# One hybrid decoder layer on one core: Strassen halves for the large input projections, token-row form everywhere

## The chip, the cores and the metric

The kernel runs on one core of one Trainium2 chip. The metric is the device time of one execution in microseconds, median over several executions of the same program. All inputs lie in the device's HBM, the weights (264 MB) among them, and stream through the core once.

## The reference, cut to what matters

One layer, 256 tokens, model width 2048, four branches of width 1024, everything in float32. `w_in` has 14 sections of 1024 columns, 324 columns of the indexer, and four gates of 2048 columns.

```python
xn = rms_norm(x, ln_g)
(a_q, a_k, a_v, a_g, c_b, c_c, c_h, c_g, s_q, s_k, s_v, s_g, m_q, m_g,
 i_q, i_k, i_w, r_a, r_c, r_s, r_m) = [xn @ w for w in cols]
y_a = moba_attention(a_q, a_k, a_v) * silu(a_g)              # causal, 8 heads of 128
y_c = c_b * short_conv(c_c * c_h, conv_w, conv_b) * silu(c_g)
y_s = dsa_attention(s_q, s_k, s_v, i_q, i_k, i_w) * silu(s_g)  # top 64 keys by the indexer
mk, mv = split(rms_norm(mem, mem_ln_g) @ w_mem_kv)
y_m = memory_attention(m_q, mk, mv) * silu(m_g)              # 4 heads of 256, 256 memory tokens
merged = (sigmoid(r_a) * (y_a @ w_branch[0]) + sigmoid(r_c) * (y_c @ w_branch[1])
          + sigmoid(r_s) * (y_s @ w_branch[2]) + sigmoid(r_m) * (y_m @ w_branch[3]))
out = rms_norm(x + merged @ w_out, final_g)
```

## The kernel before, in words

Each float32 product is made of three TensorE products of split numbers: a value is `hi` (its rounded part) plus `lo` (the rest), and hi·hi, hi·lo and lo·hi are accumulated in PSUM. The activations `x_hl` stay in SBUF in split form, the contraction (2048) on the partitions in 16 chunks `k` of 128. The weights come in tiles `raw` of 1 MB (128 partitions x 2048 numbers), each by one DMA of SP's queue (L115), into the pool `rawp` of 3 buffers. Each half of such a tile is cast by ACT to a `hi` (L99) and subtracted by DVE to a `lo` (L100); the pool `spl` holds four `hi` and four `lo` half tiles. TensorE (PE) follows.

There are two forms of a projection. In the transposed form (`project_t`, L132 and L133) the weights are the stationary operand and the tokens move: one matmul of 512 columns takes `hi` times both parts of the tokens, one of 256 columns takes `lo` times their hi; the two sums are added when they leave PSUM (`sum_t`, L149 and L150). It gives columns on the partitions, as the attention's q and k want them. In the token-row form (`project`, L156 to L158) the tokens are stationary and three matmuls of 512 weight columns move through; it gives tokens on the partitions. Before, `project_t` makes A_Q, A_K, A_G, C_B, C_C, C_H, C_G, S_Q, S_K, S_G, M_Q, M_G, the memory keys and the indexer; `project` makes the values (`to_values`), the gates of the branches ("r" in `merge_branch`), the branch outputs ("w") and the output projection ("o"). PSUM is divided into tags: `acc` 4 banks, `s` 2, `pp` and `yp` one each.

The program is written branch by branch: memory, S, A, C. A scheduler orders the instructions on each engine from there, so that a later projection's matmuls stand between those of an attention; semaphores keep data and buffers. The startup takes M_Q's first 512 columns while x arrives (`first_columns`), loads the memory (`load_mem`), squares x (`square_sums`, L180, with loads of its own through SP's queue), and then makes the memory keys (`to_heads("kt", w_mem_k, ...)`).

Of the kernel before, what the change touches and what calls it, by code (L numbers as in the profile page):

```python
# [12 lines left out]
ALU = mybir.AluOpType  # L13
# [32 lines left out]
def hybrid_kernel(ctx, tc, x, xT, mem, memT, ln_g, mem_ln_g, w_t, w_n, w_idx, conv_w, conv_b, w_mem_k, w_mem_v,  # L46
# [6 lines left out]
    rawp = ctx.enter_context(tc.tile_pool(name="rawp", bufs=3))  # L53
# [6 lines left out]
    def bank(name, tag="acc"):  # L60

        return banks.tile([P, NB], F32, name=name, tag=tag, bufs={"acc": 4, "s": 2}.get(tag, 1))
# [67 lines left out]
    def products_t(o, hi, lo, k, nk, act):  # L130

        nc.tensor.matmul(o, lhsT=hi, rhs=act(k), start=(k == 0), stop=False)  # L132
        nc.tensor.matmul(o[:, 1], lhsT=lo, rhs=act(k)[:, 0], start=False, stop=(k == nk - 1))  # L133

    def project_t(src, act):

        nk, c = src.shape[1:]
        acc = [halves(bank("acc")) for _ in range(0, c, P)]
# [6 lines left out]
    def sum_t(dst, acc, row=None, rows=P):  # L145

        for j, a in enumerate(acc):
            low = tmp.tile([P, T], F32, name="low")
            nc.scalar.copy(out=low[:rows], in_=a[:rows, 1])  # L149
            nc.vector.tensor_add(dst[:, j], a[:rows, 0], low[:rows])  # L150
            if row is not None:
                nc.vector.tensor_mul(dst[:, j], dst[:, j], row[:rows])
# [7 lines left out]
    def project(srcs, act, name, t_outer=False):  # L160

        nk = srcs[0].shape[1]
        acc = [[bank(name)[:, :src.shape[2]] for src in srcs] for t in range(2)]
        parts = [split_weights(src, src.shape[2]) for src in srcs]
        if t_outer:
            held = list(parts[0])
            steps = ((p, t, 0) for t in range(2) for p in held)
        else:
            steps = ((p, t, n) for k0 in range(0, nk, 4) for n in range(len(srcs))
                     for p in itertools.islice(parts[n], 4) for t in range(2))  # L170
        for (hi, lo, k), t, n in steps:
            a = act(k)[:, :, t * P:(t + 1) * P]
            products(acc[t][n], a[:, 0], a[:, 1], hi, lo, k == 0, k == nk - 1)
        return acc

# [37 lines left out]

    def to_gate(c0):
        dst = to_heads("gt", w_sec(c0), x_act)
        for b in range(2):
            s = dst[:, 4 * b:4 * b + 4]
            nc.scalar.activation(out=s, in_=s, func=AF.Silu)
        return dst

    def to_values(srcs, act, col=None):

        dst = big.tile([P, 2, W], F32, name="vv", tag="vv")
        for n in range(2):
            acc = project([srcs[n]], act, "v")
            for t in range(2):
                d = dst[:, t, n * NB:(n + 1) * NB]
                if col is None:
                    nc.scalar.copy(out=d, in_=acc[t][0])
                else:  # L230
                    nc.vector.tensor_scalar(d, acc[t][0], col[:, t:t + 1], None, op0=ALU.mult)
        return dst

    def gate_y(yp, gt, y, c):

        yt = tmp.tile([P, 2, T], F32, name="yt", tag="yt")
# [22 lines left out]
    def masked_attention(q, k, v, gt, mask):  # L259
        y = y_parts()  # L260
        scale = P ** -0.5
        yp = None
        for h in range(8):
# [27 lines left out]
            if h % 2 == 1:  # L291
                gate_y(yp, gt, y, h - 1)
        return y

    def memory_attention(q, k, v, gt):
        y = y_parts()
        scale = 256 ** -0.5
        for h in range(4):
# [26 lines left out]
            gate_y(yp, gt, y, 2 * h)  # L325
        return y


    def indexer_parts():
        acc = project_t(w_idx[:, :, 0:TB], x_act)  # L330
        iq = const.tile([P, 2, T], F32, name="iq")
        sum_t(iq, acc)
        acc = project_t(w_idx[:, :, TB:], x_act)
        ikw = const.tile([68, 1, T], F32, name="ikw")
        sum_t(ikw, acc, rows=68)
        ikw = ikw[:, 0]
        ikp = const.tile([P, 2, T], F32, name="ikp")
# [41 lines left out]
    def merge_branch(b, y, after=None):  # L379
# [5 lines left out]
        for j in range(2):  # L385
            sig = big.tile([P, 2, W], F32, name="sig", tag="m16b")
            for i in range(2):
                acc = project([w_n[GATES + 4 * b + 2 * j + i]], x_act, "r")
                for t in range(2):
                    nc.scalar.activation(out=sig[:, t, i * NB:(i + 1) * NB], in_=acc[t][0], func=AF.Sigmoid)  # L390
            for i in range(2):
                n = 2 * j + i
                acc = project([w_branch[b, n]], lambda k: y[:, k], "w")
                for t in range(2):
                    m = merged[:, t, n * NB:(n + 1) * NB]
                    g = sig[:, t, i * NB:(i + 1) * NB]
                    if first:
                        nc.vector.tensor_mul(m, acc[t][0], g)
                    else:
                        nc.vector.tensor_mul(g, acc[t][0], g)  # L400
                        nc.vector.tensor_add(m, m, g)
                if after is not None:
                    after(n, merged)


    def first_columns(c0, dst):

        src = w_t[FIRST[c0]:FIRST[c0] + 2].rearrange("b p k c -> p k b c")
        outs = [halves(bank("first", tag)) for tag in ("acc", "acc", "s", "s")]
        xraw = big.tile([P, KC, T], F32, name="xraw", tag="m16b")  # L410
        for k0 in range(0, KC, 4):
            raw = raw_tile(NB).rearrange("p k (b c) -> p k b c", b=2)
            n = 1 if k0 == 0 else 2
            for k in range(k0, k0 + 4, n):
# [3 lines left out]
                for i in range(n):  # L418
# [13 lines left out]
    first_columns(M_Q, q)  # L432
# [14 lines left out]
    for b in range(2, 4):  # L447
        acc = project_t(w_sec(M_Q)[b], x_act)
        load_mem(b - 2)
        sum_t(q[:, 2 * b:2 * b + 2], acc)  # L450
    for t in range(2):
        square_sums(x, t, x_ss)
    x_col, x_row = inv_rms(x_ss, "x")
    nc.vector.tensor_mul(q, q, rows(x_row, 8))
    for b in (2, 3):
        load_mem(b)
    def normalize(b):
# [4 lines left out]
        nc.vector.tensor_mul(xn, xn, rows(x_row, 4))  # L462
        split(x_hl[:, ks, 0], x_hl[:, ks, 1], xn)

    k = to_heads("kt", w_mem_k, m_act, normalize)
    m_col, m_row = inv_rms(m_ss, "m")
    nc.vector.tensor_mul(k, k, rows(m_row, 8))
    v = to_values([w_mem_v[0], w_mem_v[1]], m_act, m_col)
    gt = to_gate(M_G)
    y = memory_attention(q, k, v, gt)  # L470
    idx = indexer_parts()
    merge_branch(BR_M, y)


    mask_s = indexer(*idx)
    q = to_heads("qt", w_sec(S_Q), x_act)
    k = to_heads("kt", w_sec(S_K), x_act)
    v = to_values([w_n[V_S], w_n[V_S + 1]], x_act)
    gt = to_gate(S_G)
    y = masked_attention(q, k, v, gt, mask_s)  # L480
    merge_branch(BR_S, y)


    q = to_heads("qt", w_sec(A_Q), x_act)
    k = to_heads("kt", w_sec(A_K), x_act)
    v = to_values([w_n[V_A], w_n[V_A + 1]], x_act)
    gt = to_gate(A_G)
    y = masked_attention(q, k, v, gt, mask_a)
    merge_branch(BR_A, y)


    cc = to_heads("qt", w_sec(C_C), x_act)
    u = big.tile([P, 8, T + 2], F32, name="u", tag="kt")
    nc.gpsimd.memset(u[:, :, 0:2], 0.0)
    for b in range(4):
        acc = project_t(w_sec(C_H)[b], x_act)
        us, cs = u[:, 2 * b:2 * b + 2, 2:], cc[:, 2 * b:2 * b + 2]
        sum_t(us, acc)
        nc.vector.tensor_mul(us, us, cs)
# [6 lines left out]
    bt = to_heads("vv", w_sec(C_B), x_act)  # L506
    for b in range(2):
        s = slice(4 * b, 4 * b + 4)
# [97 lines left out]
```

## Time and profile before

| | us |
|---|---|
| median of 3 runs | 1422.03 (1420.96 to 1423.45) |
| the profiled execution | 1421.22 |
| its span, first to last instruction | 1419.4 |
| PE busy, of the span | 1402.2 (99%) |
| DVE busy | 829.2 (58%) |
| ACT busy | 698.6 (49%) |
| mean granted TensorE clock | 0.995 |

The profile lists one execution. "Busy" of PE is modelled from pipelined matmuls: a single one is listed with 0.39 us though the next begins 0.23 us later, so the pitch from start to start is the cost. The chain of waits is the path followed back from the last instruction. A window gives the busy time of each engine in a stretch.

### The profile page before, as it was taken

The numbers are of one execution on the slowest core, as the hardware profiler recorded it, in microseconds if no ns is written. First come the engines' busy times: TensorE is split into PE (matmuls) and PEld (weight loads), VectorE is DVE, ScalarE is ACT, GpSimd is POOL, SyncE is SP. The second block draws the span as 40 slices with busy tenths as digits, with TensorE's granted clock in tenths as the row PEclk, the third lists the DMA queues.
The fourth block names the chain that finished last, engine by engine and source line by source line (L and its number), as shares of the span: only waits on it lengthen the run. The fifth ranks groups of instructions, "written<-read, shape, count | busy, mean of one in ns | idle before, by whom it ended". The sixth has DMA issues, their size and how long they took to land.

```text
span 1419.4 us, 18005 instructions
## 1 busy us (share of the span) xinstructions
PE 1402.2 (99%) x7168; PEld 1189.8 (84%) x7168; DVE 829.2 (58%) x1080; ACT 698.6 (49%) x960; POOL 10.8 (1%) x25
## 2 busy tenths in 40 slices
PE   9799999999999999999999999999999999999997
PEld 8688888888888888888888888888888888888887
DVE  7775546685554446764555446764557655455654
ACT  7644356644444447734444456844444445434443
POOL 1000000000000000000000000000000000000000
PEclk9899999999999999999999999999999999999999
DMA  9765544555555555455555554455555666555553
GB/s 316 277 214 201 180 138 178 178 178 183 198 183 181 202 181 172 154 178 196 189 181 193 189 181 175 152 183 199 182 193 189 207 217 224 184 191 193 178 188 109
DMA packets 49956, 269.27 MB, mean 190 GB/s; under 512 B 6656, under 2 KB 17456, under 8 KB 19024
## 3 DMA queue, kind: packets, MB, share of 16 engines
q1 hardware_dynamic: 48960, 264.03, 54.9%
q0 software_dynamic: 624, 3.31, 0.6%
q8 instruction: 56, 0.92, 0.3%
q10 hardware_dynamic: 288, 0.79, 0.1%
q14 instruction: 28, 0.23, 0.0%
HBM read 265.88 MB, written 2.10 MB: 189 GB/s over the span
## 4 chain that ended last, share of the span: by engine, by line
PE 97%; DMA 1%; issue 0%; ACT 0%; DVE 0%; POOLq 0%; POOL 0%; DVEq 0%; SPq 0%; ACTq 0%
PE acc L132 27%; PE acc L133 14%; PE r L157 8%; PE r L156 8%; PE r L158 8%; PE w L157 4%; PE w L158 4%; PE w L156 4%; PE v L158 3%; PE v L157 3%; PE v L156 3%; PE o L158 2%; PE o L157 2%; PE o L156 2%; PE first L132 1%; DMA raw<-in_w_mem_k 1%
## 5 line engine op out<-in xcount | busy, mean ns | idle before, releaser
L100 DVE TENSOR_TENSOR lo<-raw,hi 128x1024 fp32r<-128x1024 f32 (+1 forms) x496 | 594.6, 1201 | 505.9 <-ACT hi L99 504.4
L99 ACT CAST hi<-raw 128x1024 fp32r<-128x1024 f32 (+1 forms) x496 | 510.4, 1032 | 585.1 <-PE acc L132 212.9
L132 PE MATMUL acc<-x_hl,hi 128*128 128x512 f32 x1520 | 537.2, 398 | 0.0
L133 PE MATMUL acc<-x_hl,lo 128*128 128x256 f32 x1520 | 427.5, 282 | 0.0
L132 PEld LDWEIGHTS acc<-x_hl,hi 128*128 128x128 f32 x1520 | 285.4, 188 | 70.5
L133 PEld LDWEIGHTS acc<-x_hl,lo 128*128 128x128 f32 x1520 | 284.8, 187 | 0.6
L157 PE MATMUL r<-lo,x_hl 128*128 128x512 f32 x512 | 201.8, 394 | 0.0
L156 PE MATMUL r<-hi,x_hl 128*128 128x512 f32 x512 | 201.2, 394 | 0.0
L158 PE MATMUL r<-hi,x_hl 128*128 128x512 f32 x512 | 201.1, 393 | 0.0
L156 PEld LDWEIGHTS r<-hi,x_hl 128*128 128x128 f32 x512 | 96.3, 188 | 19.9
L158 PEld LDWEIGHTS r<-hi,x_hl 128*128 128x128 f32 x512 | 96.3, 188 | 19.6
L157 PEld LDWEIGHTS r<-lo,x_hl 128*128 128x128 f32 x512 | 96.4, 188 | 19.1
L157 PE MATMUL w<-lo,y 128*128 128x512 f32 x256 | 100.0, 392 | 0.0
L158 PE MATMUL w<-hi,y 128*128 128x512 f32 x256 | 98.8, 392 | 0.0
L156 PE MATMUL w<-hi,y 128*128 128x512 f32 x256 | 98.4, 391 | 0.0
L149 ACT COPY low<-acc 128x256 f32<-128x256 f32 (+1 forms) x103 | 38.4, 374 | 76.7 <-PE acc L133 76.7
L157 PEld LDWEIGHTS w<-lo,y 128*128 128x128 f32 x256 | 48.1, 188 | 9.7
L158 PEld LDWEIGHTS w<-hi,y 128*128 128x128 f32 x256 | 48.1, 188 | 9.7
L156 PEld LDWEIGHTS w<-hi,y 128*128 128x128 f32 x256 | 48.0, 188 | 9.5
L158 PE MATMUL o<-hi,mt 128*128 128x512 f32 (+1 forms) x160 | 55.4, 347 | 0.0
L157 PE MATMUL o<-lo,mt 128*128 128x512 f32 (+1 forms) x160 | 55.2, 346 | 0.0
L156 PE MATMUL o<-hi,mt 128*128 128x512 f32 (+1 forms) x160 | 55.0, 344 | 0.0
(186 smaller groups left out, 1226.4 us busy)
## 6 DMA issues: line engine op xcount, KB each, us to landing
raw<-in_w_t SPq DMA_DIRECT2D x92, 1024.0 KB, 5.2
raw<-in_w_n SPq DMA_DIRECT2D x80, 1024.0 KB, 4.9
raw<-in_w_branch SPq DMA_DIRECT2D x32, 1024.0 KB, 5.1
raw<-in_w_out SPq DMA_DIRECT2D x16, 1024.0 KB, 4.9
raw<-in_w_mem_k SPq DMA_DIRECT2D x8, 1024.0 KB, 7.1
raw<-in_w_mem_v SPq DMA_DIRECT2D x8, 1024.0 KB, 4.8
raw<-in_w_t SPq DMA_DIRECT2D x16, 256.0 KB, 5.7
raw<-in_memT SPq DMA_DIRECT2D x2, 1024.0 KB, 6.2
```

The source lines that it names most:

```text
L99: nc.scalar.copy(out=hi, in_=src)
L100: nc.vector.tensor_sub(out=lo, in0=src, in1=hi.bitcast(F32))
L132: nc.tensor.matmul(o, lhsT=hi, rhs=act(k), start=(k == 0), stop=False)
L133: nc.tensor.matmul(o[:, 1], lhsT=lo, rhs=act(k)[:, 0], start=False, stop=(k == nk - 1))
L149: nc.scalar.copy(out=low[:rows], in_=a[:rows, 1])
L156: nc.tensor.matmul(o, lhsT=ah, rhs=hi, start=start, stop=False)
L157: nc.tensor.matmul(o, lhsT=ah, rhs=lo, start=False, stop=False)
L158: nc.tensor.matmul(o, lhsT=al, rhs=hi, start=False, stop=stop)
```

## The change

The contraction of 18 column blocks of 1024 is cut (S_Q, S_K, S_V, A_Q, A_K, A_V, C_C, C_H, C_G, C_B, and two blocks of each of the four branch gates). Chunks 0 to 7 are taken as a 2 x 2 by 2 x 2 product of blocks (two token halves, two contraction quarters, two column halves) by seven products of 12 matmuls (m1, m5, m6, m7, z, x, y) where eight stood; chunks 8 to 15 stay plain. The sums of activations are made once (`sums_of`, into `x_sums`). The sums of weights are made for each block: `bs` = b11 + b12' is a load of SP (L177) onto which a DMA of POOL's queue accumulates a second quarter (L183); DVE adds b22 onto it (L243) and later b21 (L258). `b12` is made by a load and a second accumulating DMA. Seven results pass through adds of DVE (L246, L250 to L252, L264, L270) and one copy of ACT (L239). Such a block is called a unit below.

All blocks but M_Q, the memory keys and the indexer now have the token-row form. Those that feed heads are transposed afterwards by PE (`transposed`, L334, 16 transposes of 128 x 128 for a section), and the output gates are applied after the attention (`gated`). The transposed form that is left takes three matmuls of 256 columns (L133 to L135). `rawp` has 4 buffers, PSUM's tags are `a` and `b` with 2 banks each in the place of `acc`. At the startup the squares of x, its normalization and half the memory's loads are written beside the memory keys.

```diff
-    rawp = ctx.enter_context(tc.tile_pool(name="rawp", bufs=3))
+    rawp = ctx.enter_context(tc.tile_pool(name="rawp", bufs=4))
...
     def products_t(o, hi, lo, k, nk, act):
-        nc.tensor.matmul(o, lhsT=hi, rhs=act(k), start=(k == 0), stop=False)
-        nc.tensor.matmul(o[:, 1], lhsT=lo, rhs=act(k)[:, 0], start=False, stop=(k == nk - 1))
+        a = act(k)
+        nc.tensor.matmul(o, lhsT=hi, rhs=a[:, 0], start=(k == 0), stop=False)
+        nc.tensor.matmul(o, lhsT=hi, rhs=a[:, 1], start=False, stop=False)
+        nc.tensor.matmul(o, lhsT=lo, rhs=a[:, 0], start=False, stop=(k == nk - 1))
...
+    def quarter_sum(src1, src2, k0, k1):
+        raw = quarter(src1, k0)
+        nc.gpsimd.dma_start(out=raw, in_=src2[:, k1:k1 + 4], accum_op=ALU.add)
+        return raw
...
+    def by_halves(srcs, act, sums, nat, done):
...
+        b11 = quarter(srcs[0], 0)
+        m1 = bank("m1", tag)
+        product(m1, a(0, 0), b11, True, True)
+        bs = quarter_sum(srcs[0], srcs[1], 0, 0)
+        nc.scalar.copy(out=n00, in_=m1)
+        m5 = bank("m5", tag)
+        product(m5, s(0), bs, True, True)
+        b22 = quarter(srcs[1], 4)
+        nc.vector.tensor_add(bs, bs, b22)
+        m6 = bank("m6", other)
+        product(m6, s(1), bs, True, True)
+        nc.vector.tensor_add(n01, m6, n00)
+        b12 = quarter_sum(srcs[1], srcs[1], 0, 4)
+        m7 = bank("m7", tag)
+        product(m7, s(2), b12, True, True)
+        nc.vector.tensor_add(n10, m7, n01)
+        nc.vector.tensor_add(n01, m5, n01)
+        nc.vector.tensor_add(n11, m5, n10)
+        z = bank("z", other)
+        product(z, s(3), b22, True, False)
+        r = bank("r", other)
+        plain((z, r), act, srcs[1], 8, (False, True), False)
+        b21 = quarter(srcs[0], 4)
+        nc.vector.tensor_add(bs, bs, b21)
+        y = bank("y", tag)
+        x = bank("x", tag)
+        product(x, a(1, 1), bs, True, False)
+        plain((z, r), act, srcs[1], 12, (False, False), True)
+        for t, (o, i) in enumerate(((n01, z), (n11, r))):
+            nc.vector.tensor_sub(out=o, in0=i, in1=o)
+            done(t, 1, o, False)
+        product(y, a(1, 0), b21, True, False)
+        for k0 in (8, 12):
+            plain((y, x), act, srcs[0], k0, (False, False), k0 == 12)
+        for t, (o, i) in enumerate(((n00, y), (n10, x))):
+            nc.vector.tensor_add(o, i, o)
+            done(t, 0, o, False)
...
+    def columns(c0, nat, done, halved, srcs=None):
...
+        if halved:
+            return by_halves(srcs, x_act, x_sums, nat, done)
...
-    for t in range(2):
-        square_sums(x, t, x_ss)
...
+    beside = {0: [lambda: square_sums(x, 0, x_ss)], 1: [lambda: square_sums(x, 1, x_ss), x_norm],
+              2: [lambda: normalize(0), lambda: load_mem(2)], 3: [lambda: normalize(1), lambda: load_mem(3)]}
...
+    q = to_heads("qt", S_Q, True)
+    k = to_heads("kt", S_K, True)
+    v = to_values(S_V, True)
+    masked_attention(q, k, v, mask_s)
+    finish(BR_S, S_G, q, True)
```

Where the orders stand against each other, three places matter. The first is DVE in the middle of the C branch, before, where C_H follows C_C (`lo` is half a weight tile, `qt` and `u` the two sections' sums):

```order
L100 TENSOR_TENSOR lo_8571<-raw_8548,hi_8570 128x1024 [waits PE_49,Activation_49]
L150 TENSOR_TENSOR qt_8133<-acc_8411,low_8499 128x256 [waits Activation_49]
L100 TENSOR_TENSOR lo_8602<-raw_8599,hi_8601 128x1024 [waits DMAHW2_49,PE_49,Activation_49]
L100 TENSOR_TENSOR lo_8622<-raw_8599,hi_8621 128x1024 [waits PE_49,Activation_49]
L100 TENSOR_TENSOR lo_8644<-raw_8641,hi_8643 128x1024 [waits DMAHW3_49,PE_49,Activation_49]
L150 TENSOR_TENSOR u_8502<-acc_8504,low_8590 128x256 [waits Activation_49]
```

The same engine at the same place after the change, from the last quarter of C_C's unit into C_H's (`raw_8644` is C_H's `bs`, `raw_8669` its b22, `raw_8694` its b12, `uu` C_C's result, `ch` C_H's):

```order
L100 TENSOR_TENSOR lo_8650<-raw_8644,hi_8649 128x1024 [waits DMASW0_49,Activation_49]
L270 TENSOR_TENSOR uu_8312<-y_8472,uu_8312 128x512 [waits PE_49]
L270 TENSOR_TENSOR uu_8312<-x_8473,uu_8312 128x512 [waits PE_49]
L100 TENSOR_TENSOR lo_8660<-raw_8644,hi_8659 128x1024 [waits Activation_49]
L243 TENSOR_TENSOR raw_8644<-raw_8644,raw_8669 128x2048 [waits DMAHW7_49,DVE_49]
L100 TENSOR_TENSOR lo_8674<-raw_8644,hi_8673 128x1024 [waits PE_49,Activation_49]
L100 TENSOR_TENSOR lo_8684<-raw_8644,hi_8683 128x1024 [waits PE_49,Activation_49]
L100 TENSOR_TENSOR lo_8699<-raw_8694,hi_8698 128x1024 [waits DMASW1_49,Activation_49]
L100 TENSOR_TENSOR lo_8709<-raw_8694,hi_8708 128x1024 [waits Activation_49]
L100 TENSOR_TENSOR lo_8723<-raw_8669,hi_8722 128x1024 [waits Activation_49]
L246 TENSOR_TENSOR ch_8620<-m6_8672,ch_8620 128x512 [waits PE_49]
```

Between the subtractions there now stand adds that wait for PE's end of the last unit (L270) and an add of a whole tile (L243), and two of the subtractions wait for an accumulating DMA (DMASW0, DMASW1). PE after the change, where m6 and m7 of C_H's unit meet:

```order
L154 MATMUL m6_8672<-hi_8673,x_sums_1518 128x512 [waits Activation_49]
L155 MATMUL m6_8672<-lo_8674,x_sums_1518 128x512 [waits DVE_49]
L156 MATMUL m6_8672<-hi_8673,x_sums_1518 128x512
L154 MATMUL m6_8672<-hi_8673,x_sums_1518 128x512
L155 MATMUL m6_8672<-lo_8674,x_sums_1518 128x512
L156 MATMUL m6_8672<-hi_8673,x_sums_1518 128x512
L154 MATMUL m6_8672<-hi_8683,x_sums_1518 128x512 [waits Activation_49]
L154 MATMUL m7_8697<-hi_8698,x_sums_1518 128x512 [waits Activation_49]
L155 MATMUL m6_8672<-lo_8684,x_sums_1518 128x512 [waits DVE_49]
```

The first matmul of m7, on the cast of the accumulated b12, has come to stand ahead of m6's last five. SP's loads for the same unit, with the buffers' releases they wait for:

```order
L177 DMA raw_8621<-in_w_n 128x2048 [waits DMAHW5_49,DMAHW2_49,DVE_49]
L177 DMA raw_8644<-in_w_n 128x2048 [waits DMAHW1_49,DVE_49]
L177 DMA raw_8669<-in_w_n 128x2048 [waits DMAHW7_49,DMAHW3_49,DVE_49]
L177 DMA raw_8694<-in_w_n 128x2048 [waits DMAHW4_49,DVE_49]
L177 DMA raw_8743<-in_w_n 128x2048 [waits DMAHW5_49,DVE_49]
L177 DMA raw_8777<-in_w_n 128x2048 [waits DMASW1_49,DVE_49]
```

Before, each load stood alone for its tile; now the loads of `raw_8644` and `raw_8694` are followed by an accumulation on POOL's queue, and the load of b21 (`raw_8777`) waits for the second of these.

## Rows read from the trace of the kernel before

**Rows 1.** Page, parts 1 and 4: busy time of each engine; the chain by engine.

```profile
PE 1402.2 (99%) x7168; PEld 1189.8 (84%) x7168; DVE 829.2 (58%) x1080; ACT 698.6 (49%) x960; POOL 10.8 (1%) x25
PE 97%; DMA 1%; issue 0%; ACT 0%; DVE 0%; POOLq 0%; POOL 0%; DVEq 0%; SPq 0%; ACTq 0%
```

**Rows 2.** Windows: us, busy time and instructions of PE, PEld, DVE, ACT, POOL; PEclk, DMA share, GB/s.

```profile
40.00:80.00 40.00, 31.75 (x169) 27.09 (x168) 29.24 (x38) 25.52 (x36) 1.46 (x2) 0.87 0.74 265
560.00:600.00 40.00, 40.00 (x208) 33.94 (x207) 30.69 (x69) 31.03 (x68) 0.00 (x0) 1.00 0.46 152
1200.00:1240.00 40.00, 40.00 (x177) 32.90 (x176) 17.55 (x15) 19.13 (x20) 0.00 (x0) 1.00 0.63 221
```

**Rows 3.** Timeline of PE at 985 us, row form: start, us, engine, line, operation.

```profile
985.34 0.39 PE L158 MATMUL r<-hi,x_hl 128*128 128x512 f32 x1
...
988.07 0.39 PE L158 MATMUL w<-hi,y 128*128 128x512 f32 x1
```

**Rows 4.** Timeline of PE at 43 us, transposed form.

```profile
43.51 0.40 PE L132 MATMUL acc<-x_hl,hi 128*128 128x512 f32 x1
43.74 0.28 PE L133 MATMUL acc<-x_hl,lo 128*128 128x256 f32 x1
...
49.16 0.40 PE L132 MATMUL acc<-x_hl,hi 128*128 128x512 f32 x1
```

**Rows 5.** Timeline of PE at 561 us, 256-column matmuls inside a row-form projection.

```profile
561.38 0.28 PE L252 MATMUL s<-part 128*128 128x256 f32 x1
561.50 0.28 PE L253 MATMUL s<-part 128*128 128x256 f32 x1
561.62 0.39 PE L157 MATMUL r<-lo,x_hl 128*128 128x512 f32 x1
```

**Rows 6.** Chain of waits at 207 us: start, us, what (transposes of the memory attention).

```profile
207.23 0.44 PE pp L317 x4
```

**Rows 7.** Chain of waits, startup.

```profile
42.44 6.88 DMA raw<-in_x
49.40 2.01 ACT raw L180 x2
51.43 7.57 DMA raw<-in_w_mem_k
```

**Rows 8.** Windows of the startup; columns as in rows 2.

```profile
52.00:60.00 8.00, 0.43 (x2) 0.19 (x2) 6.15 (x8) 5.82 (x9) 1.14 (x2) 0.66 0.90 320
60.00:70.00 10.00, 9.88 (x45) 8.52 (x46) 9.84 (x10) 6.29 (x8) 0.00 (x0) 0.76 0.58 204
```

**Rows 9.** Timelines at 59 and 997 us: operations in pairs, and a wait of PE.

```profile
59.02 2.00 ACT L99 CAST hi<-raw 128x1024 fp32r<-128x1024 f32 x2 [1.31 <-DMA raw<-in_w_mem_k]
60.10 2.36 DVE L100 TENSOR_TENSOR lo<-raw,hi 128x1024 fp32r<-128x1024 f32 x2
60.12 1.22 PE L132 MATMUL acc<-m16a,hi 128*128 128x512 f32 x2 [7.22 <-ACT hi L99]
...
996.85 1.28 DVE L400 TENSOR_TENSOR sig<-w,sig 128x512 f32<-128x512 f32 x2
```

**Rows 10.** Groups of DVE by form: xcount | busy, mean ns | idle before.

```profile
L100 DVE TENSOR_TENSOR lo<-raw,hi 128x1024 fp32r<-128x1024 f32 x476 | 582.0, 1225 | 498.6 <-ACT hi L99 497.3
L400 DVE TENSOR_TENSOR sig<-w,sig 128x512 f32<-128x512 f32 x24 | 15.7, 684 | 1.2 <-PE w L158 1.2
L504 DVE SCALAR_TENSOR_TENSOR qt<-u,cw,qt 128x256 f32<-128x256 f32 x16 | 6.7, 479 | 0.0
L502 DVE TENSOR_SCALAR qt<-u,cw,cb 128x256 f32<-128x256 f32 x8 | 3.0, 410 | 0.1
L454 DVE TENSOR_TENSOR qt<-qt,x_row 128x2048 f32<-128x2048 f32 x1 | 2.3, 2292 | 0.0
```

**Rows 11.** Waits: engine and tile, released by: us in total, times, longest.

```profile
DVE lo L100 <- ACT hi L99: 504.4, 402, 4.1
ACT hi L99 <- PE acc L132: 212.9, 131, 2.6
```

**Rows 12.** A queue (packets, MB, share of 16 engines); DMA issues (x, KB, us to landing).

```profile
q1 hardware_dynamic: 48960, 264.03, 54.9%
raw<-in_w_n SPq DMA_DIRECT2D x80, 1024.0 KB, 4.9
xr<-in_x POOLq DMA_DIRECT2D x2, 1024.0 KB, 6.5
```

**Rows 13.** Window in which the loads run closest; columns as in rows 2.

```profile
20.00:26.00 6.00, 6.00 (x38) 5.31 (x37) 3.29 (x6) 2.63 (x6) 0.00 (x0) 1.00 1.05 414
```

More of the change, by code (lines that the diff above doesn't have):

```diff
@@ L143, in project_t, with copy_t @@
         return acc
-    def sum_t(dst, acc, row=None, rows=P):
+    def copy_t(dst, acc, rows=P):
         for j, a in enumerate(acc):
[L148 to L152, printed above, removed]
+            nc.scalar.copy(out=dst[:, j], in_=a[:rows])
     def products(o, ah, al, hi, lo, start, stop):
@@ L158, in products, with project @@
         nc.tensor.matmul(o, lhsT=al, rhs=hi, start=False, stop=stop)
[L160 to L164, printed above, removed]
+    def project(src, act, name, t_outer=False):
+        nk, c = src.shape[1:]
+        tag = next(turn)
+        acc = [bank(name, tag)[:, :c] for t in range(2)]
+        parts = split_weights(src, c)
@@ new lines, in kept, with done, through, times @@
+    def kept(nat):
+        def done(t, n, src, psum):
+            if psum:
+                nc.scalar.copy(out=part(nat, t, n), in_=src)
+        return done
+    def through(nat, func):
+        def done(t, n, src, psum):
+            nc.scalar.activation(out=part(nat, t, n), in_=src, func=func)
+        return done
+    def times(nat, dst):
+        def done(t, n, src, psum):
+            nc.vector.tensor_mul(part(dst, t, n), src, part(dst, t, n))
+        return done
+    def transposed(nat, done):
+        for c in range(0, 8, 2):
+            pp = halves(bank("tp", "s"))
+            for i in range(2):
+                for t in range(2):
+                    nc.tensor.transpose(pp[:, i, t * P:(t + 1) * P], nat[:, t, (c + i) * P:(c + i + 1) * P], ident)
+            done(c, pp)
@@ L377, in hybrid_kernel, with gate_columns, merge @@
     state = {"merged": None}
[L379 removed]
+    def gate_columns(b, j, halved):
+        sig = nat_tile("sig")
+        columns(None, sig, through(sig, AF.Sigmoid), halved, [w_n[FIRST[R_0] + 4 * b + 2 * j + n] for n in range(2)])
+        return sig
+    def merge(b, j, sig, y, after=None):
         first = state["merged"] is None
@@ L466, in hybrid_kernel @@
+    k = big.tile([P, 8, T], F32, name="kt", tag="kt")
+    for b in range(4):
+        acc = project_t(w_mem_k[b], m_act)
+        for step in beside[b]:
+            step()
+        copy_t(k[:, 2 * b:2 * b + 2], acc)
     m_col, m_row = inv_rms(m_ss, "m")
     nc.vector.tensor_mul(k, k, rows(m_row, 8))
[L468 to L475, printed above, removed]
@@ new lines, in hybrid_kernel, with finish @@
+    for n in range(2):
+        acc = project(w_mem_v[n], m_act, "v")
+        normalize(2 + n)
+        for t in range(2):
+            nc.vector.tensor_scalar(part(v, t, n), acc[t], m_col[:, t:t + 1], None, op0=ALU.mult)
+    x_sums = big.tile([P, 4, 4, 2, P], F32R, name="x_sums", tag="m16b")
+    sums_of(lambda k0, n: x_hl[:, k0:k0 + n], x_sums)
+    memory_attention(q, k, v)
+    def finish(b, gate, val, halved, after=None):
+        y = to_gate(gate, val, False) if gate is not None else val
+        for j in range(2):
+            merge(b, j, gate_columns(b, j, halved), y, after)
@@ L493, in hybrid_kernel @@
+    columns(C_H, nat, times(nat, uu), True)
     u = big.tile([P, 8, T + 2], F32, name="u", tag="kt")
     nc.gpsimd.memset(u[:, :, 0:2], 0.0)
[L495 to L499, printed above, removed]
+    transposed(uu, lambda c, pp: nc.scalar.copy(out=u[:, c:c + 2, 2:], in_=pp))
+    cc = big.tile([P, 8, T], F32, name="cc", tag="qt")
     for c in range(8):
```

264 lines of the change are left out of this document (141 added, 123 removed).

## The prediction, made before the changed kernel ran

> **What bounds the kernel now.** I read the page first: PE is busy 99% of the span, and 97% of the chain that ended last is PE [rows 1]. Windows say where it is not: in 40 to 80 us PE is busy 31.75 of 40 us, elsewhere 40.00 of 40, with DVE at 30.69 in an attention stretch and 17.55 in a quiet one [rows 2]. So outside the startup a matmul taken away is time taken away, as long as the two engines that prepare weights keep ahead. The waits show that they do: DVE's subtraction waits 504.4 us for ACT's cast, which in turn waits 212.9 us for PE to give its buffer back [rows 11]. DVE and ACT idle because PE is slow, and the question is whether they still do after the change.
>
> **PE's work.** Prices are pitches, start to start. Row form: 12 matmuls between 985.34 and 988.07 us, 2.73 us, so 0.2275 each [rows 3]. Transposed form: 16 pairs in 43.51 to 49.16 us, 5.65 us, 0.353 a pair [rows 4]. A 256-column matmul takes 0.12 [rows 5], a transpose 0.44 / 4 = 0.11 [rows 6].
> - 18 units lose 12 of 192 matmuls: 18 x 12 x 0.2275 = -49.1 us.
> - 11 column blocks go from 128 pairs (45.2 us) to 192 row-form matmuls (43.7 us): -1.5 x 11 = -16.5 us.
> - 9 sections get 16 transposes: 144 x 0.11 = +15.8 us.
> - 304 pairs that stay transposed (M_Q 128, memory keys 128, indexer 48) become three matmuls of 0.12: 304 x 0.007 = +2.1 us.
>
> PE's work: -47.7 us, 3.4%.
>
> **Startup.** Before, SP issues the x loads and the memory loads ahead of the memory keys: the chain goes through x (6.88 us), its squares on ACT (2.01) and then the first key weights (7.57) [rows 7], and PE is busy 0.43 us in 52 to 60 us. In the 10 us after it, its granted clock is 0.76 [rows 8], a mean between its two levels, 1.2 and 2.4 GHz. The change moves the squares with their two loads, the normalization and two memory loads beside the key projections; the key weights go out behind the first half of the memory. Idle 7.6 us and 10 x (1 - 0.76) = 2.4 us at a low clock: -10 us. The moved steps are not free: each load is one more place in SP's queue (1 MB in 2.53 us at 414 GB/s [rows 13]), and DVE and ACT do the same work later, beside 180 us of matmuls that leave DVE idle. Next late would be the key weights themselves; ends 0 and -10, I take -10, since the chain names just the loads that go. `sums_of` adds two tile-half adds, four smaller ones and four splits, some 7 us of DVE once, beside the memory attention: nothing.
>
> **DVE in a unit.** Two casts in a row take 2.00, one 1.05, so a step of 0.95; two subtractions take 2.36 [rows 9], a lone one 1.225 [rows 10], so a step of 1.14. A 128x512 operation takes 0.684 alone [rows 10] and two take 1.28, so a step of 0.60 [rows 9]; a 128x2048 operation 2.29 [rows 10], less the same 0.08 in a row, 2.21. Per block before: 16 x 1.14 = 18.2 of 43.7 us. Per unit now: 22 x 1.14 + 2 x 2.21 + 8 x 0.60 = 34.3 of 180 x 0.2275 = 41.0 us. It still fits, by 6.7 us. But it is not even. The order excerpt of DVE shows what stands between the end of one unit and m6 of the next: two adds that wait for PE's last matmul (1.2), the second half of m5 (1.14), the add of b22 (2.21), then ACT's cast (1.05) and the subtraction (1.23): 6.8 us. PE has m1 and m5 in that time and the first matmul of m6, 25 x 0.2275 = 5.69. Stall per unit: 1.1 us, with semaphores (0.06 between cast and subtraction's start [rows 9]) 1.3. Everything queued behind the add of b22 on DVE (both halves of m6, then of m7) shifts with it; who waits is PE.
>
> Ten units are quiet. Eight have other DVE work in them: the first units of S and A (indexer, transposes' copies), the gates beside the attentions, and C_G with the convolution, 16 x 0.479 + 8 x 0.410 = 10.9 us [rows 10], 4.2 more than the spare. I take 4 us for each of the eight, with ends of 1.3 (it hides) and 8 (it comes in a lump in front of m6): 10 x 1.3 + 8 x 4 = **+45 us**, ends 23 and 77.
>
> ACT per unit: 22 x 0.95 and some 1 us of copies, 22 of 41 us: nothing, its cover is PE's 41.
>
> **The DMA chain.** Before, loads take 54.9% of 16 engines [rows 12]. A unit brings 9 loads and 2 accumulations, 11 MB in 41 us, 27.8 us at the closest pace of 2.53: no bandwidth problem. It's the latency: in SP's order b12's load goes into a buffer that comes free about 8.6 us before the unit's m1 (counted along the order with the pitches above); it lands 4.9 us or more after its issue [rows 12], about 1.2 us before m1, as it shares the engines with its neighbours; only then does POOL's accumulation go out. PE needs m7's cast, by the order excerpt in the middle of m6, 31 matmuls and the stall after m1's start: 7.05 + 1.2 - 1.05 for the cast = 7.2 us. No accumulating DMA exists before. The nearest row is POOL's plain load of 1 MB, 6.5 us [rows 12]: it would land about 4.9 us after m1 (4.7 to 5.3, as the load lands), 2.3 us to spare. That's one end. The other: an accumulation moves twice the data (old and added operand both read), 6.5 + 2.5 = 9.0 us; and because `bs`'s accumulation stands before it on POOL's queue, and its buffer delays the load behind it, b12 is late by twice 2.5 = 5.0, which is 2.7 us beyond the spare. The 10 units that stand back to back pay it: **+27 us**; the eight gate units follow 96 to 192 plain matmuls and don't. A price below that of the plain load has nothing for it: it also writes 1 MB. I take 9.0, since an add must read what it adds to.
>
> The Trainium skill has a rule that speaks here ("Collectives: The Full Stack", section "The bandwidth ceiling: the fold count and why AG ≠ RS ≠ AR"): a reducing transfer needs two source reads on one ring, and was measured 62.28 / 32.35 = 1.93 times slower than a copy. No run of before shows it; it is a rule on rings between cores. By it alone an accumulation would be an estimated 1.93 x 2.53 = 4.9 us of engine time, which gives the second end again.
>
> Also on POOL's in-order queue: 36 accumulations, each of which waits for its load; the indexer's two 64 KB copies and the x loads for the end stand behind them, both with 40 us or more before they're needed: nothing. The output's gate now comes after the attention and the transposes stand before "w"; a gate unit stands between, so nothing.
>
> **Sum.** Against the profiled execution, 1421.2 us (0.8 under the median): 1421.2 - 47.7 - 10 + 45 + 27 = 1435.5; **1436 us** against the median, 1% slower. About 0.2% is what a measurement of this kernel can tell from no change.
>
> **Rivals.**
> - A, *accumulation at the plain price*: b12 lands 2.3 us ahead of need, the +27 goes; 1421.2 - 47.7 - 10 + 45 = 1409 us, faster. With all of DVE's extra work hidden (23): 1387. It decides at an accumulation of about 7.7 us, (2 x (7.7 - 6.5) = the spare of 2.3). For it: the DMA engines are half idle [rows 12], and a second read can run beside the write. Against: the load behind which it queues already takes 4.9 us where 2.53 is the pace.
> - B, *the DMA queues become the bound*: 264.03 MB are 252 loads of 1.049 MB; 54.9% of 1419.4 us [rows 12] over 252 is 3.09 us of engine time each, 0.56 more than the 2.53 of the closest window. With 13 passes for a unit (9 loads, 2 accumulations of two) that is 40.2 of 41 us: no lost microsecond is caught up. b12 comes behind five passes of its unit and its own load, 6 x 0.56 = 3.4 us later, in all 18 units: 1435.5 + 60 = 1495 us. Against: in the startup 414 GB/s were reached [rows 13].
> - C, *the startup doesn't shrink*: the key weights were late because the memory itself was; +10 on any of the above. It moves the time inside the other ranges and has no chance of its own.
>
> **Chances.** Forecast 0.42 (1420 to 1455 is its own range: the ends of DVE's term with each other term as taken, cut where they'd overlap A and B), A 0.42 (1385 to 1421), B 0.16 (1455 to 1510). The rows bear out A and the forecast equally: one price decides, and none of the rows has it; B is contradicted by the closest window. The range 1385 to 1485 leaves out the top of B and the case in which no DVE lump shows at all. Within 0.2%: 0.03 of A's and 0.03 of the forecast's share, 0.06; faster 0.40 (A, and 0.01 of the forecast); slower 0.54.
>
> **What the profile after would show.** Right: PE 1354 us or so busy; idle of PE in front of m6's second matmul (L155), released by DVE's `lo`, and in front of m7's first (L154), released by ACT's cast which itself waited for an accumulating DMA (L183); L183's landing at about 9 us; DVE's busy share near 80%; the transposes (L334) at 0.11 and no gap in 52 to 60 us. Rival A: L183 lands under 7.7 us and PE never waits for m7. Rival B: the share of the DMA queues above 85%, and PE waiting for plain loads (L177) as well. I'd be wrong altogether if DVE's adds of whole tiles took far from 2.2 us, if PE's clock fell in the stalls (it is 1.00 in both later stretches [rows 2]), or if the scheduler's order left PE behind a wait that neither engine nor DMA explains.

## The result, and the profile after

The changed kernel takes 1465.74 us (median of 4, 1464.31 to 1472.70) where the one before took 1422.46 beside it: ratio 1.0315, 95% interval 1.028 to 1.035. The profiled execution is 1464.31 us. The forecast was 1436: the sign was right, the size a third of what came, and the time lies inside the range. All comparisons below are with the median 1465.7. The edited versions were run once each, except e15 and e16 (four times); the four runs of the changed kernel spread over 8 us, so a gain of 8 to 11 us of a single run (e8, e11, e14) is at the edge of what can be told.

The page of the changed kernel, parts 1, 3, 4 and 6 (answering to [rows 1, 12]):

```profile
span 1462.5 us, 17425 instructions
PE 1387.2 (95%) x6696; PEld 1145.2 (78%) x6696; DVE 1072.8 (73%) x1277; ACT 789.8 (54%) x1028; POOL 42.5 (3%) x61
...
q1 hardware_dynamic: 51552, 282.90, 54.5%
q0 software_dynamic: 5808, 41.06, 14.3%
...
PE 61%; DMA 17%; DVE 15%; ACT 4%; issue 3%; POOLq 0%; POOL 0%; ACTq 0%; DVEq 0%
...
raw<-in_w_n POOLq DMA_DIRECT2D x36, 1024.0 KB, 9.4
```

PE's part of the chain that ended last fell from 97% to 61%; DMA and DVE have 32% of it. Where PE stood is in part 5, by operation and releaser (`m` is m1, m5, m6 and m7 together):

```profile
L154 PE MATMUL m<-hi,x_sums 128*128 128x512 f32 x216 | 91.5, 434 | 27.0 <-ACT hi L99 26.4
L155 PE MATMUL m<-lo,x_sums 128*128 128x512 f32 x216 | 95.1, 440 | 19.8 <-DVE lo L100 19.7
L155 PE MATMUL x<-lo,x_hl 128*128 128x512 f32 x216 | 85.2, 395 | 3.2 <-DVE lo L100 2.7
L154 PE MATMUL x<-hi,x_hl 128*128 128x512 f32 x216 | 85.0, 394 | 2.2 <-ACT hi L99 2.2
```

The idle time is in front of the products with weight sums, and hardly any in front of x. Idle time is counted only from a matmul's listed end. Counted from start to start against the pitch of 0.2275, over 512-column matmuls that follow each other, PE loses 46 us in front of and within m6, 17 at m5 and 6 at m7, some 100 in all; in all of these counts m5, m6 and m7 are told apart by their order on PE.

What a stall is made of shows in the chain of waits of the changed kernel where C_C's unit ends and C_H's begins (m1 of C_H starts at 1068.9 us; pieces under 0.05 us are left out):

```profile
1058.95 12.51 DMA raw<-in_w_n
1071.56 1.05 ACT hi L99
1072.63 0.98 DVE lo L100
1073.62 0.16 issue
1073.78 1.28 DVE uu L270 x2
1075.06 1.14 DVE lo L100
1076.22 2.30 DVE raw L243
1078.61 1.05 ACT hi L99
1079.68 1.24 DVE lo L100
1080.96 0.80 PE m L155
```

`bs`'s accumulation goes out at 1058.95 and lands 12.51 us later. Only then does the row of the prediction begin, and it is longer by its first two steps (cast and subtraction of m5's first half), since these too waited. PE on the same stretch:

```profile
1071.40 0.39 PE L156 MATMUL m<-hi,x_hl 128*128 128x512 f32 x1
1072.65 0.50 PE L154 MATMUL m<-hi,x_sums 128*128 128x512 f32 x1 [0.86 <-ACT hi L99]
1073.92 0.51 PE L155 MATMUL m<-lo,x_sums 128*128 128x512 f32 x1 [0.76 <-DVE lo L100]
...
1076.25 0.50 PE L155 MATMUL m<-lo,x_sums 128*128 128x512 f32 x1 [0.66 <-DVE lo L100]
...
1077.29 0.40 PE L156 MATMUL m<-hi,x_sums 128*128 128x512 f32 x1
1079.70 0.80 PE L154 MATMUL m<-hi,x_sums 128*128 128x512 f32 x1 [2.02 <-ACT hi L99]
1080.96 0.80 PE L155 MATMUL m<-lo,x_sums 128*128 128x512 f32 x1 [0.47 <-DVE lo L100]
```

It waits for m5 (1072.65, 1073.92, and 1076.25 for the second half), then for m6 (1079.70, 1080.96). Windows of the startup and of that stall (columns as in rows 2):

```profile
52.00:60.00 8.00, 8.00 (x73) 8.00 (x72) 4.73 (x6) 4.95 (x5) 1.29 (x1) 1.00 0.77 279
60.00:70.00 10.00, 10.00 (x90) 10.00 (x89) 4.57 (x4) 5.54 (x7) 0.34 (x1) 1.00 0.57 197
1079.00:1083.00 4.00, 2.83 (x6) 1.94 (x7) 3.15 (x3) 3.47 (x4) 0.00 (x0) 0.51 0.31 64
```

The startup's gap [rows 8] is gone. After the idle in front of m6 the granted clock is at its lower level, 1.2 GHz (0.51 of 2.4).

### The profile page after: what moved, and what is told of

The parts are those of the page before. It is cut to its first block, busy times and chain, and to the rows that moved or that the text cites. A ratio compares the mean times of both kernels' runs of the same rounds, so it can differ in the third digit from the quotient of the medians.

```text
span 1462.5 us, 17425 instructions
## 1 busy us (share of the span) xinstructions
PE 1387.2 (95%) x6696; PEld 1145.2 (78%) x6696; DVE 1072.8 (73%) x1277; ACT 789.8 (54%) x1028; POOL 42.5 (3%) x61
## 3 DMA queue, kind: packets, MB, share of 16 engines
q1 hardware_dynamic: 51552, 282.90, 54.5%
q0 software_dynamic: 5808, 41.06, 14.3%
## 4 chain that ended last, share of the span: by engine, by line
PE 61%; DMA 17%; DVE 15%; ACT 4%; issue 3%; POOLq 0%; POOL 0%; ACTq 0%; DVEq 0%
DMA raw<-in_w_n 16%; DVE lo L100 8%; PE r L155 4%; PE r L156 4%; PE r L154 4%; ACT hi L99 4%; PE x L155 2%; PE x L156 2%; PE x L154 2%; PE y L154 2%; PE y L156 2%; PE y L155 2%; PE w L155 2%; PE w L154 2%; PE w L156 2%
## 5 line engine op out<-in xcount | busy, mean ns | idle before, releaser
L100 DVE TENSOR_TENSOR lo<-raw,hi 128x1024 fp32r<-128x1024 f32 (+1 forms) x604 | 712.9, 1203 | 347.7 <-ACT hi L99 345.3
L99 ACT CAST hi<-raw 128x1024 fp32r<-128x1024 f32 (+1 forms) x604 | 613.3, 1035 | 584.0 <-PE x L156 90.1
L155 PE MATMUL r<-lo,x_hl 128*128 128x512 f32 x336 | 132.8, 395 | 0.0
L154 PE MATMUL r<-hi,x_hl 128*128 128x512 f32 x336 | 132.2, 394 | 0.0
L156 PE MATMUL r<-hi,x_hl 128*128 128x512 f32 x336 | 132.0, 393 | 0.0
L154 PE MATMUL m<-hi,x_sums 128*128 128x512 f32 x216 | 91.5, 434 | 27.0 <-ACT hi L99 26.4
L155 PE MATMUL m<-lo,x_sums 128*128 128x512 f32 x216 | 95.1, 440 | 19.8 <-DVE lo L100 19.7
L156 PE MATMUL m<-hi,x_sums 128*128 128x512 f32 x216 | 89.5, 414 | 0.0
L155 PE MATMUL x<-lo,x_hl 128*128 128x512 f32 x216 | 85.2, 395 | 3.2 <-DVE lo L100 2.7
L154 PE MATMUL x<-hi,x_hl 128*128 128x512 f32 x216 | 85.0, 394 | 2.2 <-ACT hi L99 2.2
L154 PE MATMUL y<-hi,x_hl 128*128 128x512 f32 x216 | 84.7, 392 | 0.0
L156 PE MATMUL x<-hi,x_hl 128*128 128x512 f32 x216 | 84.6, 392 | 0.0
L156 PE MATMUL y<-hi,x_hl 128*128 128x512 f32 x216 | 84.6, 392 | 0.0
L155 PE MATMUL y<-lo,x_hl 128*128 128x512 f32 x216 | 84.4, 391 | 0.0
L154 PEld LDWEIGHTS r<-hi,x_hl 128*128 128x128 f32 x336 | 63.1, 188 | 12.5
```

The costliest lines, as they stand in the source:

```text
L99: nc.scalar.copy(out=hi, in_=src)
L100: nc.vector.tensor_sub(out=lo, in0=src, in1=hi.bitcast(F32))
L154: nc.tensor.matmul(o, lhsT=ah, rhs=hi, start=start, stop=False)
L155: nc.tensor.matmul(o, lhsT=ah, rhs=lo, start=False, stop=False)
L156: nc.tensor.matmul(o, lhsT=al, rhs=hi, start=False, stop=stop)
```

## The experiments

Theory D: DVE's row in front of m6 is the loss, as the prediction's +45 had it. Theory Q: the accumulations are, bs's above all. The first three leave out sums, the fourth the units.

**e1**, no accumulations:

```diff
-        nc.gpsimd.dma_start(out=raw, in_=src2[:, k1:k1 + 4], accum_op=ALU.add)
```


> Leaves out the accumulation of the second quarter onto bs and b12 (36 DMAs of 1 MB), so the products m5, m6, m7 and x are taken of other weight sums than the algorithm's; all matmuls, casts, subtractions and DVE adds stay. Theory D (the stall in front of m6 comes from DVE's row: adds that wait for the last unit, the add of b22, cast, subtraction): only what stands in front of m5 and m7 goes, some 15 to 20 us of 1464, so 1445 to 1450, and m6 still stalls 2.4 us or more in every unit. Theory Q (bs's accumulation lands late, shifts m5 and with it everything behind): the ten units that stand back to back fall to the 1.3 us that the DVE row alone gives, 45 us or more go, 1405 to 1420.

**e2**, no tile adds of DVE:

```diff
-        nc.vector.tensor_add(bs, bs, b22)
-        nc.vector.tensor_add(bs, bs, b21)
```


> Leaves out DVE's two adds of whole tiles for each unit (b22 and b21 onto bs); the accumulations stay. Theory D: the row in front of m6 is 2.2 us shorter than what PE has to do in that time, its stall goes nearly everywhere; 50 us or more go, 1405 to 1415. Theory Q: m5 still waits for bs (15 us in all) and m6 behind it; under 30 us go, 1435 or more.

**e3**, both edits:

> Leaves out both: the 36 accumulations and the 36 adds of whole tiles. If the weight sums are the whole loss in m5, m6 and m7 (some 75 us with the half clock behind the stalls), 1380 to 1390 under either theory: 1421 - 47.7 - 10 = 1364 plus what stalls elsewhere (x, z, attention, indexer, some 20 us). Where the two single gains add up to more than this one, either cause alone already hides the other.

**e4**, in `columns`:

```diff
-        if halved:
+        if False:
```


> All 18 blocks plain (192 matmuls), so no sums and no seven products; the token-row form, the transposes, the later gates, four raw buffers and the new startup stay. By the terms of the prediction: 1421 - 16.5 + 15.8 + 2.1 - 10 = 1412 to 1413. A rival: the transposes and later gates stall PE, 1420 or more.

Measured: e1 1415.3, e2 1439.0, e3 1368.3, e4 1409.7, with 1423.2 before beside them. So e1 fell as Q had it, by 50, e2 by 27, and both together by 97, more than the sum of the two. e3 lies 12 under the expected 1380 to 1390, e4 2 under its 1412 to 1413. In e3's groups next to nothing is left in front of the sums' products:

```profile
L155 PE MATMUL m<-lo,x_sums 128*128 128x512 f32 x216 | 85.6, 396 | 0.0
L154 PE MATMUL m<-hi,x_sums 128*128 128x512 f32 x216 | 82.5, 398 | 1.4 <-ACT bg L238 1.4
```

In e1's there are 19 us, with DVE's row by itself:

```profile
L155 PE MATMUL m<-lo,x_sums 128*128 128x512 f32 x216 | 89.7, 415 | 11.1 <-DVE lo L100 11.1
L154 PE MATMUL m<-hi,x_sums 128*128 128x512 f32 x216 | 86.7, 412 | 7.9 <-ACT hi L99 7.1 <-ACT nkt L238 0.4 <-ACT bg L238 0.3
```

With DVE's adds, accumulations cost 50; without them, 71 (e2 less e3). So each hides some 20 us of the other, and e2 shows where. Counted from start to start as above, PE loses 24 us at m5, 8 in m6 and 28 at m7 in e2. There b12 comes late too, and in the changed kernel the stall in front of m6 covers it. This is the first matmul of m7 in A_Q's unit of e2, in the chain of waits and in PE's timeline:

```profile
678.30 8.47 DMA raw<-in_w_n
...
686.87 1.05 ACT hi L99
...
687.97 0.50 PE m L154
```

```profile
687.97 0.50 PE L154 MATMUL m<-hi,x_sums 128*128 128x512 f32 x1 [2.90 <-ACT hi L99]
```

e4 says that token rows, transposes and the new startup are worth 13.5 us by themselves.

**e5**, the second DMA copies:

```diff
-        nc.gpsimd.dma_start(out=raw, in_=src2[:, k1:k1 + 4], accum_op=ALU.add)
+        nc.gpsimd.dma_start(out=raw, in_=src2[:, k1:k1 + 4])
```


> The second DMA onto bs and b12 stays, from the same queue, behind the same load, with the same 1 MB, but copies in place of adding (so m5, m6, m7 and x are taken of other weights). Without any second DMA the time was 1415, with the accumulating one 1464. Theory P (the price: an accumulation moves its data twice and lands in 9.4 us where a copy takes about 6.5): most of the 49 us go, 1415 to 1430. Theory S (the series: two transfers one behind the other, whatever the second does, with the buffer waits around them): little goes, 1445 to 1460. By the prediction's rival A, 1409.

1428.9: theory P. The price is what decides, 37 of the 50 us. The line of POOL's second DMAs (L183) in the changed kernel, minimum, median and maximum of the time to landing, with who waited for it:

```profile
  ACT hi L99: 73.5, 21
...
DMA to landing us min/median/max: 7.9/9.4/13.0
```

The same line of e5:

```profile
DMA to landing us min/median/max: 5.0/6.7/9.8
```

POOL's queue in e5 (packets, MB, share of 16 engines), to be set beside the 14.3% above:

```profile
q0 software_dynamic: 5808, 41.06, 7.6%
```

Without second DMAs (e1) that queue has 0.7% of 16 engines' span. So 36 accumulations take (14.3 - 0.7)% x 1462.5 / 36 = 5.53 us of it each, 36 copies (7.6 - 0.7)% x 1427.1 / 36 = 2.74: twice. The rule of the Trainium skill ("Collectives: The Full Stack", section "The bandwidth ceiling: the fold count and why AG ≠ RS ≠ AR") is one on rings between cores; its 1.93 for a reducing transfer against a copy agrees with the 5.53 / 2.74 = 2.02 here.

Which accumulation? **e13** takes bs's away, **e14** b12's:

```diff
-        bs = quarter_sum(srcs[0], srcs[1], 0, 0)
+        bs = quarter(srcs[0], 0)
```


> Leaves out the accumulation onto bs alone (m5, m6 and x are taken of other weights); b12's stays. Without both the time was 1415, with both 1464. As the prediction had it (b12 alone is late): under 10 us go, 1455 or more. If bs is what is late (the stalls in front of m5, and m6 behind the add that waits for it): 30 us or more go, 1420 to 1435.

```diff
-        b12 = quarter_sum(srcs[1], srcs[1], 0, 4)
+        b12 = quarter(srcs[1], 0)
```


> Leaves out the accumulation onto b12 alone (m7 is taken of other weights); bs's stays. As the prediction had it: 27 us or more go, 1437 or less. If bs is what is late: b12's lateness is hidden behind m6's stall, under 15 us go, 1450 or more. If the two gains of these runs add up to less than 49, each lateness hides the other.

1427.4 and 1456.0: 38 and 10 of the 50, both as expected if bs is what is late. It is bs. In the changed kernel's POOL row, taken one by one, bs's accumulations land after 8.6 to 13.0 us (median 11.1), b12's after 7.9 to 11.2 (median 8.2). By issues and landings, 1.3 plain loads on average are in flight beside one of bs's and 0.3 beside one of b12's; no run tests whether that makes the difference.

**e17** moves bs's load and accumulation one buffer ahead:

```diff
+        bs = quarter_sum(srcs[0], srcs[1], 0, 0)
         b11 = quarter(srcs[0], 0)
...
-        bs = quarter_sum(srcs[0], srcs[1], 0, 0)
```


> Same arithmetic and work; only the load and accumulation of bs are written ahead of b11's load, so that they go out one buffer earlier, some 3 to 5 us. If the place in the order is the cause of bs's lateness: most of the 37 us that leaving it out gave, 1425 to 1440. If what runs beside it (or b11's load, now behind) is: 1455 or more.

1441.1, just over the band: 25 us of the 38 come back by the place alone. Landings got no shorter (7.9 / 9.6 / 14.8); what changed is when they begin.

**DVE's row.** **e6** writes z's product in front of m6, **e8** makes the tile adds in two halves, **e10** lets DVE make all four sums, **e11** issues each accumulation in two halves, **e12** is e6, e8 and e11 together, **e18** that with e17.

```diff
+        z = bank("z", other)
+        product(z, s(3), b22, True, False)
         m6 = bank("m6", other)
```


> Same arithmetic; the product z, whose weights (b22) need no sum, is written between m5 and m6, 2.73 us of PE's work in which b22 can be added onto bs. Of the 47 us that DVE's adds cost without accumulations, stalls of 2.4 to 2.7 us a unit should go; what bs's late landing costs in front of m5 stays, and b12 has 2.7 us more. If both work: 1400 to 1420. If the late landings only come out elsewhere, 1440 or more.

```diff
-        nc.vector.tensor_add(bs, bs, b22)
+        for h in (0, 2):
+            nc.vector.tensor_add(bs[:, h:h + 2], bs[:, h:h + 2], b22[:, h:h + 2])
```


> Same arithmetic; DVE's two adds of whole tiles are made in two halves each, so that the cast of m6's first half can begin 1.1 us earlier. Where DVE's row sets m6's stall, 1.1 us a unit go: 18 x 1.1 = 20, so 1440 to 1448. If the landing of bs sets it all, under 10 us.

```diff
-        nc.gpsimd.dma_start(out=raw, in_=src2[:, k1:k1 + 4], accum_op=ALU.add)
+        nc.vector.tensor_add(raw, raw, quarter(src2, k1))
```


> Same arithmetic; the two accumulating DMAs of each unit are undone: the second quarter is a plain load into a buffer of its own, and DVE adds it, so all four weight sums are DVE's. DVE then has 34.3 + 2 x 2.2 = 38.7 of 41 us, the DMA queues 11 plain passes. Against 1464: theory P (the accumulation's price) 1435 to 1455, since DVE's row in front of m6 gets 2.2 to 4.4 us longer as the late landings go; if DVE becomes the bound, 1465 to 1490.

```diff
+        for h in (0, 2):
+            nc.gpsimd.dma_start(out=raw[:, h:h + 2], in_=src2[:, k1 + h:k1 + h + 2], accum_op=ALU.add)
```


> Same arithmetic; each accumulating DMA is issued as two of 512 KB, so that the cast of the first half can begin when the first has landed. If an accumulation's time is its data (5.5 us of 16 engines) plus a fixed part, the first half lands some 2 to 3 us earlier: m5 and m7 wait less, 1445 to 1457. If the second half's landing decides (through DVE's add of b22), 1458 to 1466.

> Same arithmetic; z in front of m6 (alone 1437, -27), DVE's tile adds in two halves (alone 1457, -8) and the accumulations in two halves. If the three work on different waits, 1464 - 27 - 8 - 10 = 1419; where z already covers the row in front of m6, the other two add nothing, 1430 to 1437.

> Same arithmetic; z first, halves of adds and accumulations, bs ahead, all 18 blocks as units: without bs ahead 1422. If the section units' stalls come from bs's place, 1400 to 1412; if they come from DVE's row and the buffers, within 5 us of 1422.

e6 1437.3, e8 1456.5, e10 1468.6, e11 1454.9, e12 1422.4, e18 1409.9. e6 missed its band by 17: z covers m6 (17 us lost there, 46 before), but part of the wait moves on to z itself (18 us, 6.5 before). e8 gave 9, as its second theory had it (bs's landing sets the stall), where the first had 20. e10 is in the band of its second theory, though DVE is 79% busy and not full: its longer row in front of m6 costs 67 us there. The accumulating DMAs, late as they are, are no worse than DVE making the sums. e11 is in its first band. The gains of e6, e8 and e11 nearly add up (28 + 9 + 11 = 48; e12 gave 43), as if they worked on different waits. e18 is in its first band: with z first and the halves, bs's place is worth another 12.5 us.

**e7** and **e9** put a unit's plain quarters between its products; e9 also x and its add behind y:

```diff
+        plain((z, r), act, srcs[1], 8, (True, True), (False, False))
         b11 = quarter(srcs[0], 0)
...
-        m6 = bank("m6", other)
+        plain((z, r), act, srcs[1], 12, (False, False), (False, True))
+        m6 = bank("m6", tag)
```


> Same arithmetic; a unit begins with a plain quarter (chunks 8 to 11, 5.5 us of PE), then m1 and m5, then the second plain quarter (5.5 us), then m6, m7, z. Each wait for a sum gets 5.5 us of cover: the accumulation of bs is needed later after its load, the add of b22 has 5.5 us before m6, b12 as much. If the loss is latency in the wrong place, as both theories say, nearly all of it goes: 1370 to 1395, under both kernels and under the plain blocks' 1410. If the DMA engines' or DVE's work as such is too much (rival B), 1430 or more.

> Same arithmetic; as the version with plain quarters between (1506), but DVE's add of b21 and the product x that needs it stand behind y and one more plain quarter. In that version DVE, in order, stood at the add of b21, whose load waited for b12's buffer, with z's subtractions behind it, and PE lost 94 us in front of z. Theory S (the loss is the place of a late transfer in an in-order row, not the work): that goes, 1375 to 1420. Theory W (the work: 4 buffers of which two are held for long, DMA queues with 38 of 41 us per unit): z is free but others stall, 1440 or more.

1506.3 and 1508.6, the worst of all. The times lie in the bands of "work" (1430 or more, 1440 or more), but what stalls is z (94 us of PE in e7, 90 in e9), which neither expectation had. b12's accumulation now goes out late, 7.5 to 11.8 us after m1's start where it was 4.9 ahead to 4.3 behind. DVE in e9, beside C_C's unit, whose b12 accumulation went out at 1069.50 and landed 9.3 us later:

```profile
1072.25 3.64 DVE L100 TENSOR_TENSOR lo<-raw,hi 128x1024 fp32r<-128x1024 f32 x3
1080.22 1.22 DVE L100 TENSOR_TENSOR lo<-raw,hi 128x1024 fp32r<-128x1024 f32 x1 [4.33 <-ACT hi L99]
1081.37 2.28 DVE L266 TENSOR_TENSOR raw<-raw 128x2048 f32<-128x2048 f32 x1
1083.57 2.35 DVE L100 TENSOR_TENSOR lo<-raw,hi 128x1024 fp32r<-128x1024 f32 x2
```

DVE stands 4.33 us for b12's first half, and the scheduler has put the add of b21 (L266) right behind it, ahead of z's subtractions, though e9 wrote it later. So it seems that a cover for one late transfer became the delay of the next, with two of the four buffers held by bs and b22; this is read from the trace, no run tests it.

**e15** keeps e12's units for the gates alone, **e16** for every second section block as well:

```diff
-    q = to_heads("qt", S_Q, True)
+    q = to_heads("qt", S_Q, False)
...
-    columns(C_B, nat, times(nat, bg), True)
+    columns(C_B, nat, times(nat, bg), False)
```


> Same result by other products: only the eight gate blocks are units, in the order of the version with z first and the halves (1422); the ten section blocks are plain. All blocks plain gave 1410. If units that follow plain matmuls hide their sums: in the 1422 version such units last 41.9 us where plain ones take 43.7, so 8 x 1.8 = 14 us less, 1393 to 1400. If each unit pays as much as it saves, 1408 to 1412.

> As the one before, but of the ten section blocks S_Q, S_V, A_Q, A_V, C_C and C_G are units too, each behind a plain block. If a plain block ahead is all that a unit needs: 14 x 1.8 = 25 us less than 1410, 1382 to 1390. If attention, transposes and convolution beside them fill DVE's row, no better than the gates alone, 1395 to 1410.

e15: 1400.99 (1400.80 to 1404.41), ratio to before 0.986, interval 0.984 to 0.9875. e16: 1403.35 (1401.20 to 1409.43), 0.988, interval 0.985 to 0.991. Both beat both kernels and e4's single run (1409.7). e15 missed its first band by 1 us: the second gate unit of a branch takes 41.0 to 41.9 us, from its first matmul to its last, against 43.7 for a plain block, but the first one, with the branch's other work beside it, 45.0 to 53.5. e16 is in its second band: its six section units take 41.8 to 50.7 us with what stands beside them and return nothing.

## Why the prediction was right in sign and wrong in size

| term | predicted | measured, from |
|---|---|---|
| token rows, transposes, startup | -8.6 | -13.5 (e4 less before) |
| 216 matmuls fewer | -49.1 | -49.1 taken, +7.7 left over (e3 less e4) |
| DVE's adds | +45 | +47 (e1 less e3) |
| accumulations | +27 | +50 (changed less e1) |
| sum | +14 | +43 |

- **PE's work and the startup** held. The 256-column matmul accounts for the surplus of 5 us: three of them take 0.34 us in the chain of waits of the changed kernel:

```profile
29.93 0.11 PE acc L133
30.05 0.11 PE acc L134
30.16 0.11 PE acc L135
30.27 0.11 PE acc L133
```

  That is 0.113 each, where the rows gave 0.12 [rows 5]; 304 x (0.34 - 0.353) is -4 where +2.1 stood.
- **DVE's row** held: L243 takes 2.29 us, and the row is as the order excerpt had it. That +45 and +47 lie so close is partly luck. In e1, PE loses 30 us in m6, from 0.1 to 3.9 a unit, and not by the prediction's split into quiet units (1.3) and others (4, a choice between 1.3 and 8).
- **The price of an accumulation** held in the median: 9.0 taken, 9.4 measured; a plain second DMA 6.7 where 6.5 was the other end. Rival A was priced too low all the same: e5 has its price and takes 1429, not 1409. Of these 20 us, 6 are in e1 already, which has no second DMA. bs isn't what is late in the other 14: in eight of the nine units named below its copy lands 1.4 to 3.9 us ahead of m1, and PE loses 1.5 us at m5, as in e1 (1.2). They are spread (some 3 us each in m6 and at the indexer's matmuls, 2 at x) and weren't separated further.
- **The step that failed is the place of that price**: "b12 is late by twice 2.5 = 5.0" and "The 10 units that stand back to back pay it", +27 us. The prediction asked when b12 was due and never asked it of bs, which it only let pass its delay on. In nine units (S_Q, S_K, S_V, A_K, A_V, C_H, C_G, C_B and C's first gate, which the prediction took to follow plain matmuls) bs's accumulation goes out 7.7 to 10.6 us ahead of m1. m5's first matmul needs bs's cast, its second the subtraction too, so bs must have landed 2.73 + 0.23 - 1.05 - 1.23 = 0.7 us after m1: it has 8.4 to 11.2 us. The 9.0 of the prediction fit in eight of the nine. What came, 8.6 to 13.0 us there (bs's median over all units is 11.1), fits in none: bs landed 0.8 to 3.5 us after m1. Nearly all that PE loses at m5 (16 of 17 us) is in these nine. Where bs is late it stands at the head of DVE's row and shifts m6 too. Written as a term: 38 us for bs (e13), which the prediction had at nothing, and 10 for b12 (e14), which it had at 27.
- **The sum of the terms** failed with it. b12 is late as well, but the terms +45 and +27 were added as if their waits stood one behind the other. They run partly side by side: b12's lateness shows at m7 once DVE's adds are gone (28 us in e2, 6 in the changed kernel). That 28 comes near +27 is luck: 20 of them lie in six units that follow plain matmuls.
- **Rival B** did not come: the plain queue has 54.5%, and all 21 waits of ACT's casts for a w_n tile (73.5 us) are for POOL's DMAs, none for a plain load.
- **Clock.** The prediction counted on 1.00 in the stalls. The mean is 0.987 against 0.995, so (1 - 0.987) x 1462.5 = 19.0 us of full-speed time against 7.1 before: up to 12 us of the stalls' price is the lower level behind them. Of the 7.7 left over it is little: e3 has 0.998 and e4 0.999, (1 - 0.998) x 1366.5 - (1 - 0.999) x 1407.8 = 1.3 us. In e3, PE loses 6 us at z; the cause stays open.

## What to carry to other kernels

When two transfers in a series feed a sum, ask of each sum in turn when it goes out, when it lands under the load that runs beside it, and when it is due; the first of a pair is as good a suspect as the last. A late transfer at the head of an in-order row shifts the whole row, and the row's stall in turn hides what comes late further on: ask at each product which wait ends last, and don't add the waits as terms. Fewer matmuls did not pay by themselves: beside the version without units (1409.7), all 18 units as first written lost 56 us, and eight gate units with z first and the halves gave 9; six section units behind plain blocks added nothing to that.

## What the runs showed of the hardware

An accumulating DMA of 1 MB onto SBUF takes 5.53 us of 16 engines' time and lands after 9.4 (median), a copy from the same queue 2.74 and 6.7. After PE had been idle 2.02 us in front of m6, right behind shorter waits, its clock was granted 0.51 in 1079 to 1083 us, and matmuls came 0.43 us apart where 0.23 is the pitch at 2.4 GHz.
